# An expert's tokens: rows fetched from DRAM through a slot table and transposed, or columns picked by matrix products

## Chip, cores, metric

One core of a Trainium2 chip. The metric is the device time of one execution in microseconds (us), of three executions; beside it stands one execution taken by the hardware profiler. Engines: TensorE (PE, its weight loads PEld), VectorE (DVE), ScalarE (ACT), GpSimd (POOL), and SyncE (SP), which here only issues transfers. Sixteen DMA engines move the data of all queues.

## The reference, cut to what matters

A decoder of two layers over 256 tokens and 16 meta tokens, D = 1024. The second layer ends in a feed-forward of eight experts, of which each token uses two:

```python
def moe_swiglu(h, router, wg, wu, wd):
    logits = (t @ router).astype(jnp.float32)
    vals, idx = lax.top_k(logits, TOP_K)
    gates = jax.nn.softmax(vals, axis=-1)
    combine = jnp.sum(jax.nn.one_hot(idx, N_EXPERTS) * gates[..., None], 1)
    for e in range(N_EXPERTS):
        out = out + combine[:, e:e + 1] * swiglu(t, wg[e], wu[e], wd[e])
h = layer_norm(ALPHA * h + f, ln2_g[i], ln2_b[i])
```

with `swiglu(t, wg, wu, wd) = (silu(t @ wg) * (t @ wu)) @ wd` and an expert's width of 1408. All is float32; the kernel makes every float32 operand of a product into a high half and a low rest (both float32r) and adds two or three products of halves.

## The kernel before, in words

The first layer, the second layer's mixer and the router fill the time up to about 597 us. From there to about 1064 us the eight experts run one after the other; the change lies there.

**Weights.** An expert has 18 pieces ("units") of up to 1 MB: twelve of the two up products, six of the down product. SP loads them in order (`emit_load`, line 279) into landing buffers called `raw`: four of a ring, and as fifth the tile `yt` once the residual stream in it is done with (line 1562). Four more tiles (`yh`, `yl`, `hid0`, `hid1`, line 1003) serve once, for the first loads of the expert part, before they get their own content. `emit_split` (lines 293 to 327) makes a unit into a high half on ScalarE (line 318) and a low half on VectorE (line 316); after that the landing buffer is free, and the next load can start. Loads wait in SP's queue in the order of issue, so one that waits holds up all behind it.

**Order of the work.** The instructions of PE, DVE, ACT and POOL stand as the program writes them. `product(e, s, ...)` (line 1351) is one of nine phases of an expert: phases 0 to 5 are the up products (`up_proj`), 6 to 8 the down products (`down_proj`). Each takes two units. The lists `todo[e, s]` hold what stands ahead of the product, after a first split, and after a second split. A mask with two bits an expert, read into registers, says how many slots an expert has: at most 64 (one block, high and low half side by side), up to 128, or more, in which case a second block runs under `tc.If` (`second`, line 1165). Experts are sorted by their number of tokens (`order_tables`); with these inputs the third and the sixth have a second block, and the first has one full block. The other five are small.

**Tokens of an expert.** `halve_stream` (line 1246) makes the stream `yt`, 256 rows of 1024, into two tiles `halves_y`. `find` (line 1035) compares the slot numbers with the table `pmk` of each token's slot and gives a matrix of zeros and ones, `hot`. `x_pick` (line 1040) multiplies: for each of eight column blocks and each half, two matrix products of 128x128 by 128x256 give the transposed tokens of all 256 slots in PSUM, exactly, since one factor is one or zero. `x_store` (line 1053) copies them to the tiles `x`. `prepare(e)` (line 1373) spreads these 32 products over phases 4 to 8 of the expert before (`PICKS`). The first expert's tokens are picked in `x_first`, which the change leaves.

**Results.** An expert's rows are written to the DRAM tensor `ys` by POOL (`finish`, line 1500: for a small expert two writes, the second added to the first and waiting for it). At the end `fetch_results` (line 1298) gets each token's rows back by an indirect transfer, and `scale_stream` (line 1318) remakes the stream from the two halves.

```python
    def x_pick(hot, ms, bk):
        for half in range(2):
            for q, m in enumerate(ms):
                for b in range(2):
                    nc.tensor.matmul(ps[:, q, :], halves_y[half][:, b, m * P:(m + 1) * P], hot[:, b, :],
                                     start=(b == 0), stop=(b == 1))
```

Of the kernel before, what the change touches and what calls it, by code (L numbers as in the profile page):

```python
# [11 lines left out]
F32 = mybir.dt.float32  # L12
# [8 lines left out]
P = 128  # L21
# [184 lines left out]
def trunk(ctx, tc, x, meta_tokens, params, consts, selector, rows, weights, out):  # L206
# [156 lines left out]
    ys = dram.tile([2 * (NE - 1) * P, D], F32, name="ys")  # L363

# [47 lines left out]
    def prepare_bias():  # L412
# [559 lines left out]
    def rt(name, dt=F32, w=NE):  # L972
        return wk.tile([P, 2, w], dt, name=name)
# [12 lines left out]
    def y_tile(q):  # L986
        return wk.tile([P, 2, D], F32R, tag=f"y{q}", name=nm("y"), bufs=1)

    def x_tile():
        return wk.tile([P, 2, 2 * P, 2], F32R, tag="x", name=nm("x"), bufs=6)  # L990

    def x_block(xs, s):
        return lambda k: xs[k // 2][:, k % 2, s * P:(s + 1) * P, :]
# [8 lines left out]
    halves_y, hids, got, final = [], [], [], []  # L1002
    spare += [(wk, t, 0) for t in ("yh", "yl", "hid0", "hid1")]
# [6 lines left out]
    def x_first(s, xs):  # L1010
# [9 lines left out]
        for hf in range(2):  # L1020
# [8 lines left out]
            for q in range(2):  # L1029
                halve(raw[:, 2 * q:2 * q + 2, :], xs[2 * hf + q][:, :, s * P:(s + 1) * P, :], P)  # L1030
# [9 lines left out]
    def x_pick(hot, ms, bk):  # L1040

        out = bk.rearrange("p (h m t) -> p h m t", h=2, m=1) if len(ms) == 1 else None
        res = []
        for half in range(2):
            ps = out[:, half] if out is not None else bk[half].rearrange("p (m t) -> p m t", m=2)
            for q, m in enumerate(ms):
                for b in range(2):
                    nc.tensor.matmul(ps[:, q, :], halves_y[half][:, b, m * P:(m + 1) * P], hot[:, b, :],  # L1048
                                     start=(b == 0), stop=(b == 1))
            res.append(ps)  # L1050
        return res

    def x_store(ps, xs, ms):
        dst = xs[ms[0] // 2][:, ms[0] % 2:ms[0] % 2 + len(ms)]
        nc.scalar.activation(dst[:, :, :, 0], ps[0], AF.Copy)
        if len(ms) == 1:
            nc.scalar.activation(dst[:, :, :, 1], ps[1], AF.Copy)
        else:
            vec.tensor_copy(dst[:, :, :, 1], ps[1])


    mask = wk.tile([1, 1], I32, name="mask")
# [590 lines left out]
```

## Time and profile before

| | before |
|---|---|
| median of 3 executions | 1084.95 us (1084.66 to 1088.38) |
| profiled execution | 1084.34 us, span 1082.3 us |
| PE busy | 1024.9 us, 95% of the span |
| DVE busy | 816.9 us, 75% |
| ACT busy | 661.5 us, 61% |
| POOL busy | 29.9 us, 3% |
| moved by DMA | 241.01 MB, mean 223 GB/s |
| SP's weight loads (q1) | 223.72 MB, 56.4% of 16 engines |
| POOL's transfers (q0) | 15.19 MB, 4.2% |

The span runs from the first to the last instruction; the time of an execution has some 2 us more around it. A busy share is an average over stages with different limits, so the expert part is read by stretches. In rows of the trace, "out<-in" names the tiles, "xN" the number of instructions, and an arrow at the end of a row names what ended the idle time before it.

### The profile page before, as it was taken

To read this page: it belongs to the slowest core of one execution; us is meant where nothing else is said; L and a number is where in the kernel's file an instruction comes from. 1 tells how busy PE (TensorE), PEld (TensorE's weight loads), DVE (VectorE), ACT (ScalarE), POOL (GpSimd) and SP (SyncE) were. 2 spreads that over 40 slices of the span, in tenths; PEclk is the share of its full clock that TensorE was granted. 3 is DMA by queue.
4 is the path that set the end of the run, shared out by engine and by line. 5 is a ranking of instruction groups with operands and counts; after the bars stand their busy time and mean duration, and the time that the engine had idled before them with its cause. 6 is when DMAs were issued, how large, how long until landed. Compare 5 with 4: busy or idle time off the path is not lost. (4 is left out here: it accounts for less than half of the span.)

```text
span 1082.3 us, 17618 instructions
## 1 busy us (share of the span) xinstructions
PE 1024.9 (95%) x6619; PEld 926.4 (86%) x6619; DVE 816.9 (75%) x1228; ACT 661.5 (61%) x910; POOL 29.9 (3%) x49
## 2 busy tenths in 40 slices
PE   6999999999999999999999999899998989999895
PEld 3999999899999998989999777789877878978773
DVE  6799977555555545999996998965579995568996
ACT  5348664554544335458566778845569874548983
POOL 0410000000000000000000000000000000000001
PEclk9999999899999999999998999999999999999998
DMA  6962435065455451634346579974679996568994
GB/s 246 320 255 80 155 121 191 1 248 181 157 192 172 153 184 48 226 117 157 117 161 261 203 287 344 390 262 184 231 272 378 396 393 218 190 233 304 383 335 161
DMA packets 37633, 241.01 MB, mean 223 GB/s; under 512 B 4466, under 2 KB 4594, under 8 KB 13952
## 3 DMA queue, kind: packets, MB, share of 16 engines
q1 hardware_dynamic: 33120, 223.72, 56.4%
q0 software_dynamic: 4208, 15.19, 4.2%
q8 instruction: 91, 1.49, 0.5%
q10 hardware_dynamic: 176, 0.29, 0.1%
q14 instruction: 38, 0.31, 0.1%
HBM read 228.41 MB, written 10.77 MB: 221 GB/s over the span
## 5 line engine op out<-in xcount | busy, mean ns | idle before, releaser
L316 DVE TENSOR_TENSOR ws<-raw,ws 128x1024 fp32r<-128x1024 f32 (+3 forms) x307 | 487.5, 1601 | 149.2 <-ACT ws L318 143.7
L318 ACT ACTIVATE ws<-raw 128x1024 fp32r<-128x1024 f32 (+3 forms) x305 | 412.1, 1369 | 109.2 <-PE mm L527 86.1
L527 PE MATMUL mm<-hH,ws 128*128 128x272 f32 (+1 forms) x1568 | 303.2, 290 | 0.0
L527 PEld LDWEIGHTS mm<-hH,ws 128*128 128x128 f32 x1568 | 250.2, 191 | 2.2 <-issue 0.4
L1183 PE MATMUL bank<-ws,x 128*128 128x512 f32 (+1 forms) x1104 | 246.5, 380 | 5.1 <-PEq L1168 4.5
L1183 PEld LDWEIGHTS bank<-ws,x 128*128 128x128 f32 x1104 | 204.0, 192 | 39.7 <-issue 9.3
L527 PE MATMUL mm<-hL,ws 128*128 128x272 f32 (+1 forms) x784 | 226.7, 289 | 0.0
L527 PEld LDWEIGHTS mm<-hL,ws 128*128 128x128 f32 x784 | 149.2, 190 | 0.7
L1183 PE MATMUL bank<-ws,hid 128*128 128x512 f32 x506 | 124.1, 399 | 8.8 <-DVEq L1168 6.8
L1183 PEld LDWEIGHTS bank<-ws,hid 128*128 128x128 f32 x506 | 95.1, 192 | 29.0 <-issue 9.9
L597 DVE SCALAR_TENSOR_TENSOR cbuf<-cbuf,par 128x272 f32<-128x272 f32 (+1 forms) x240 | 106.9, 488 | 0.7
L527 PE MATMUL mm<-fh,ws 128*128 128x272 f32 x352 | 67.1, 289 | 0.0
L527 PEld LDWEIGHTS mm<-fh,ws 128*128 128x128 f32 x352 | 55.3, 188 | 0.1
L1409 ACT ACTIVATE t<-bank 128x512 f32<-128x512 f32 (+1 forms) x48 | 26.6, 554 | 45.1 <-PE bank L1183 43.0
L527 PE MATMUL mm<-fl,ws 128*128 128x272 f32 x176 | 50.6, 287 | 0.0
L527 PE MATMUL mm<-mH,ws 128*128 128x272 f32 (+1 forms) x256 | 49.3, 287 | 0.0
L1048 PE MATMUL bank<-hot,y 128*128 128x256 f32 x224 | 36.0, 292 | 10.7 <-DVE t L1425 6.1
L1048 PEld LDWEIGHTS bank<-hot,y 128*128 128x128 f32 x224 | 30.6, 189 | 16.5 <-DVE t L1425 8.0
L527 PEld LDWEIGHTS mm<-mH,ws 128*128 128x128 f32 x256 | 40.2, 188 | 0.2
L527 PE MATMUL mm<-mL,ws 128*128 128x272 f32 (+1 forms) x128 | 36.3, 285 | 0.0
L527 PEld LDWEIGHTS mm<-fl,ws 128*128 128x128 f32 x176 | 33.1, 188 | 0.0
L1416 PEld LDWEIGHTS bank<-fold,t 128*128 128x128 f32 x220 | 26.9, 191 | 4.0 <-ACTq L1168 2.4
(309 smaller groups left out, 1007.6 us busy)
## 6 DMA issues: line engine op xcount, KB each, us to landing
raw<-in_weights_dram SPq DMA_DIRECT2D x182, 1024.0 KB, 6.0
raw<-in_weights_dram SPq DMA_DIRECT2D x33, 768.0 KB, 6.0
raw<-in_weights_dram SPq DMA_DIRECT2D x8, 512.0 KB, 6.3
ys<-zero POOLq DMA_DIRECT2D x7, 512.0 KB, 12.4
ys<-y POOLq DMA_DIRECT2D x10, 256.0 KB, 6.8
row<-in_rows_dram POOLq DMA_DIRECT2D x2, 1024.0 KB, 7.6
ys<-zero POOLq DMA_DIRECT2D x7, 256.0 KB, 15.5
ys<-y POOLq DMA_DIRECT2D x3, 512.0 KB, 2.9
```

Source lines behind the costliest of these rows:

```text
L316: nc.vector.tensor_sub(lo[:, c0:c1], r[:, c0:c1], h[:, c0:c1].bitcast(F32))
L318: nc.scalar.activation(h[:, c0:c1], r[:, c0:c1], AF.Copy)
L527: nc.tensor.matmul(dst, ww[:, w0:w0 + P], aa[:, ks + i, n0:n1], start=(start and i == 0 and q == 0), stop=(stop and i == len(subs) - 1 and ...
L597: nc.vector.scalar_tensor_tensor(ca[:, c, n0:], src, w, ca[:, c, n0:], op0=ALU.mult, op1=ALU.add)
L1048: nc.tensor.matmul(ps[:, q, :], halves_y[half][:, b, m * P:(m + 1) * P], hot[:, b, :], start=(b == 0), stop=(b == 1))
L1183: nc.tensor.matmul(dst, a, w[:, c0:c1], start=start and q == 0, stop=stop and q == len(terms) - 1)
L1409: nc.scalar.activation(t[q][:, :n], sums[q][:, :n], AF.Copy)
L1416: nc.tensor.matmul(turned[q][:, k * P:k * P + 64], src, fold, start=True, stop=True)
```

## The change

The tokens of the second to the eighth expert are no longer picked by products.

- `keep_stream` writes the stream `yt` to a DRAM tensor `yd` (two writes on POOL, each for 128 tokens).
- `token_table` works out, for each token's two choices, a place in a DRAM table of 8 x 2 x 128 entries, and POOL scatters the tokens' numbers to these places by four indirect transfers; the table was zeroed at the start. It is then read back as `slot_ids`.
- `prepare(e)` has POOL fetch the expert's rows from `yd` by `slot_ids` into the tile `xg`: 64 rows for a small expert, 128 otherwise, and 128 more if there is a second block. TensorE transposes the eight column blocks (`x_turn`, two times four, after phases 6 and 7), and `x_store` halves them on ScalarE and VectorE. For a second block a jump decides on eight more transposes after phase 8 and their halving in the next expert's phase 0.
- `halves_y` and most of the comparisons go. Two tiles `more0`, `more1` are landing buffers that come back after each split. The tiles `x` are now one per block.
- At the end `fetch_stream` reads the stream back from `yd`, and `scale_stream` is one ScalarE instruction per 128 tokens.

```diff
+    yd = dram.tile([SEQ, D], F32, name="yd")
+    table = dram.tile([2 * NE * P, 1], I32, name="table")
...
+        nc.gpsimd.dma_start(table.rearrange("(p c) o -> p (c o)", p=P), zero[:, :2 * NE].bitcast(I32))
...
-    spare += [(wk, t, 0) for t in ("yh", "yl", "hid0", "hid1")]
+    spare += [(wk, t, 0) for t in ("hid0", "hid1")] + [(wk, f"more{i}", 1) for i in range(2)]
...
+    def x_turn(ps, s, hf):
+        for q in range(4):
+            m = 4 * hf + q
+            nc.tensor.transpose(ps[:, q * P:(q + 1) * P], xg[:, s, m * P:(m + 1) * P], ident)
+
+    def x_store(ps, xs, s, hf):
+        halve(ps.rearrange("p (k t) -> p k t", k=4), xs[s][:, 4 * hf:4 * hf + 4], P)
...
+    def token_table():
+        at = rt("at", tag="pos")
+        vec.tensor_scalar(at, pmk, P - BIG, 1.0 - 2 * NE * P, op0=ALU.is_ge, op1=ALU.mult)
+        vec.scalar_tensor_tensor(at, pmk, 2.0 * NE, at, op0=ALU.mult, op1=ALU.add)
+        vec.scalar_tensor_tensor(at, ebase, 2.0 / P, at, op0=ALU.mult, op1=ALU.add)
+        for t in range(2):
+            w, r, ri = rt(f"tw{t}", tag=f"w{t}"), rt(f"tr{t}", w=1, tag=f"gl{t}"), rt(f"ti{t}", dt=I32, w=1)
+            vec.tensor_mul(w, oh[t], at)
+            vec.tensor_reduce(r, w, axis=AX, op=ALU.add)
+            vec.tensor_scalar(r, r, 2.0 * NE * BIG, None, op0=ALU.add)
+            vec.tensor_copy(ri, r)
+            for b in range(2):
+                nc.gpsimd.indirect_dma_start(table, bass.IndirectOffsetOnAxis(ap=ri[:, b, :], axis=0),
+                                             ids[:, b:b + 1], None)
+        nc.gpsimd.dma_start(slot_ids, table.rearrange("(p c) o -> p (c o)", p=P))
...
+    def keep_stream(b):
+        nc.gpsimd.dma_start(yd[b * P:(b + 1) * P, :], yt[:, b, :])
...
+    def fetch_stream():
+        final.append(ring.tile([P, 2, D], F32, tag="yt", name=nm("stream"), bufs=1))
+        nc.gpsimd.dma_start(final[0], yd.rearrange("(b p) d -> p b d", p=P))
...
     def scale_stream(b):
-        high, low = (q[:, b, :].bitcast(F32) for q in halves_y)
-        nc.scalar.activation(stream(b), low, AF.Copy, scale=ALPHA)
-        vec.scalar_tensor_tensor(stream(b), high, ALPHA, stream(b), op0=ALU.mult, op1=ALU.add)
+        nc.scalar.activation(stream(b), stream(b), AF.Copy, scale=ALPHA)
...
+        def gather(s, n):
+            nc.gpsimd.indirect_dma_start(xg[:n, s, :], None, yd, bass.IndirectOffsetOnAxis(
+                ap=slot_ids[:n, 2 * e + s:2 * e + s + 1], axis=0))
...
+        todo[e - 1, 3 if e > 1 else 4][2].append(gathers)
+        for hf in range(2):
+            todo[e - 1, 6 + hf][1].append(lambda hf=hf: turn(hf))
+            todo[e - 1, 7 + hf][0].append(lambda hf=hf: store(hf))
+        todo[e - 1, 8][1].append(turn_second)
+        todo[e, 0][0].append(store_second)
...
+    todo[0, 1][1].append(token_table)
...
-        todo[0, 2 + b][2].append(lambda b=b: halve_stream(b))
+        todo[0, 1 + b][2].append(lambda b=b: keep_stream(b))
...
-        todo[NE - 1, 2 + b][2].append(lambda b=b: scale_stream(b))
+        todo[NE - 1, 4 + b][2].append(lambda b=b: scale_stream(b))
+    todo[NE - 1, 2][2].append(fetch_stream)
```

Where instructions stand, at three places. POOL in the first expert, before: after the loading of two parameter rows there is nothing up to the writing of the first expert's rows, of which the one or the other branch runs.

```order
L1168 UNCONDITIONAL_BRANCH
L1357 UNCONDITIONAL_BRANCH
L1505 REGISTER_ALU
L1505 COMPARE_AND_BRANCH
L1509 DMA ys<-y_7560 64x1024 [waits DMASW0_49,DVE_49,Activation_49]
```

POOL at the same place now; in brackets stand the semaphores that a row waits for (DMASW: POOL's own transfers in turn, DVE, PE, Activation: the engines).

```order
L1166 DMA table<-ids,ti_798_7026 2048x1 [waits DMASW1_49,DVE_49,Pool_49]
L1166 DMA table<-ids,ti_798_7026 2048x1 [waits DMASW2_49,DMASW1_49]
L1166 DMA table<-ids,ti_801_7035 2048x1 [waits DMASW3_49,DMASW2_49,DVE_49]
L1178 UNCONDITIONAL_BRANCH
L1166 DMA table<-ids,ti_801_7035 2048x1 [waits DMASW4_49,DMASW3_49]
L1370 UNCONDITIONAL_BRANCH
L1168 DMA slot_ids<-table 128x16 [waits DMASW5_49,DMASW4_49]
L1257 DMA yd<-yt_last 128x1024 [waits DMASW6_49,DVE_49]
L1257 DMA yd<-yt_last 128x1024 [waits DMASW7_49,DVE_49]
L1392 REGISTER_ALU
L1392 COMPARE_AND_BRANCH
L1387 DMA xg<-yd,slot_ids 64x1024 [waits DMASW6_49,DMASW7_49,DMASW5_49,DMASW0_49]
```

Seven transfers came in ahead of the first gather; each scatter waits for the semaphore of the transfer before it, and the gather for both writes of `yd` and for `slot_ids`.

SP in the first expert, before (raw_7409 goes into `yt`; DMAHW: SP's own transfers in turn):

```order
L279 DMA raw_7273<-in_weights_dram 128x2048 [waits DMAHW7_49,DMAHW3_49,DVE_49]
L1168 UNCONDITIONAL_BRANCH
L1357 UNCONDITIONAL_BRANCH
L279 DMA raw_7409<-in_weights_dram 128x2048 [waits DMAHW4_49,DVE_49,PE_49]
L1357 UNCONDITIONAL_BRANCH
L279 DMA raw_7415<-in_weights_dram 128x2048 [waits DMAHW5_49,DMAHW0_49,DVE_49]
L279 DMA raw_7421<-in_weights_dram 128x1024 [waits DMAHW6_49,DMAHW1_49,DVE_49]
```

SP there now (raw_7180 and raw_7294 go into `more0` and `more1`, raw_7435 into `yt`):

```order
L279 DMA raw_7180<-in_weights_dram 128x2048 [waits DMAHW5_49,DMAHW3_49,DVE_49]
L279 DMA raw_7294<-in_weights_dram 128x2048 [waits DMAHW6_49,DMAHW4_49,DVE_49]
L1392 UNCONDITIONAL_BRANCH
L1178 UNCONDITIONAL_BRANCH
L1370 UNCONDITIONAL_BRANCH
L279 DMA raw_7301<-in_weights_dram 128x2048 [waits DMAHW7_49,DVE_49]
L1370 UNCONDITIONAL_BRANCH
L279 DMA raw_7435<-in_weights_dram 128x1024 [waits DMASW7_49,DMASW6_49,PE_49]
L279 ISA
L279 DMA raw_7441<-in_weights_dram 128x2048 [waits DMAHW0_49,DVE_49]
```

The load into `yt` is now the expert's last unit, two loads later in the order, and waits for POOL's two writes of `yd`.

PE in the third expert, after its seventh product, before (`hot` and `y` are the factors of a pick):

```order
L1169 UNCONDITIONAL_BRANCH
L1168 UNCONDITIONAL_BRANCH
L1048 MATMUL bank_6546<-hot_9486,y_7153 128x256 x4
L1048 MATMUL bank_6543<-hot_9486,y_7154 128x256 x4
L1168 UNCONDITIONAL_BRANCH
L1357 REGISTER_ALU
L1357 COMPARE_AND_BRANCH
```

PE there now (`con` holds the identity matrix, `xg` the fetched rows):

```order
L1179 UNCONDITIONAL_BRANCH
L1178 UNCONDITIONAL_BRANCH
L1044 MATMUL bank_6549<-con,xg 128x128 x4
L1370 REGISTER_ALU
L1370 COMPARE_AND_BRANCH
L1193 MATMUL bank_6545<-ws_9921,hid_9123 128x512
```

Eight products of 256 columns became four transposes of 128; four more stand after the eighth product, and the picks at the other places of the expert are gone.

## Rows read from the trace of the kernel before

**Rows 1.** The cores view of the whole program: span and mean granted TensorE clock.

```profile
core 0: 1082.3 us, clock 0.981
```

**Rows 2.** Table by stretches: length, busy us by engine, granted clock, DMA share, GB/s.

```profile
core 0: us, PE busy (x) PEld busy (x) DVE busy (x) ACT busy (x) POOL busy (x), PEclk, DMA share, GB/s
...
612.00:620.00 8.00, 7.44 (x37) 6.11 (x36) 7.71 (x7) 5.81 (x7) 0.00 (x0) 1.00 0.34 138
620.00:628.00 8.00, 7.28 (x38) 6.41 (x37) 7.97 (x8) 3.49 (x5) 0.00 (x0) 1.00 0.01 2
...
660.00:670.00 10.00, 10.00 (x51) 8.30 (x51) 9.74 (x5) 9.06 (x7) 0.00 (x0) 1.00 0.96 326
...
720.00:797.00 77.00, 76.08 (x394) 65.62 (x393) 44.12 (x53) 40.48 (x46) 1.10 (x2) 1.00 0.58 206
...
860.00:880.00 20.00, 17.49 (x106) 15.47 (x104) 19.14 (x14) 18.35 (x21) 0.00 (x0) 1.00 1.00 394
...
895.00:979.00 84.00, 83.29 (x424) 71.53 (x423) 47.17 (x41) 43.49 (x48) 1.29 (x3) 1.00 0.59 205
...
990.00:1010.00 20.00, 18.04 (x110) 16.26 (x109) 18.68 (x15) 17.30 (x19) 0.00 (x0) 1.00 0.97 389
```

**Rows 3.** The waits of SP's queue, 590 to 1060 us: total, times, longest.

```profile
SPq L279 <- DVE ws L316: 347.2, 118, 18.4
```

**Rows 4.** Line 279's loads, 805 to 895 us: ns, first and last start; landing.

```profile
L279 SPq DMA_DIRECT2D raw<-in_weights_dram x34: 332/333/337, 807.1 to 891.2; - x34
...
DMA to landing us min/median/max: 4.8/7.2/8.8
```

**Rows 5.** The same view, 715 to 795 us.

```profile
DMA to landing us min/median/max: 4.1/4.9/6.2
```

**Rows 6.** Picks of line 1048, third and sixth expert: length, PE, PEld busy.

```profile
705.00:795.00 90.00, 4.60 (x32) 4.45 (x32) 1.00 0.63 227
...
887.00:977.00 90.00, 4.60 (x32) 4.45 (x32) 1.00 0.62 225
```

**Rows 7.** Groups of instructions by form: count, busy us, mean ns, idle before.

```profile
L1048 PE MATMUL bank<-hot,y 128*128 128x256 f32 x224 | 36.0, 292 | 10.7 <-DVE t L1425 6.1 <-issue 3.0 <-PEq L1168 0.9
...
L1059 DVE CAST x<-bank 128x512 fp32r<-128x512 f32 x21 | 14.4, 685 | 0.2 <-PE bank L1183 0.2
...
L1008 DVE TENSOR_TENSOR hid<-t,hid 128x512 fp32r<-128x512 f32 x16 | 11.0, 689 | 0.0
```

**Rows 8.** PE's timeline in the third expert: start, length (us).

```profile
742.57 1.10 PE L1048 MATMUL bank<-hot,y 128*128 128x256 f32 x8
...
747.76 1.04 PE L1418 MATMUL bank<-con,t 128*128 128x128 f32 x8
```

**Rows 9.** VectorE's timeline in the first expert.

```profile
610.80 0.17 DVE L1158 TENSOR_TENSOR chosen<-oh,oh 128x16 f32<-128x16 f32 x1
```

**Rows 10.** The writes of line 1509 (small experts, 0.26 MB), all: landing.

```profile
DMA to landing us min/median/max: 6.3/6.8/7.3
```

**Rows 11.** The writes of line 1511 (0.5 MB), all: landing.

```profile
DMA to landing us min/median/max: 2.9/2.9/7.5
```

**Rows 12.** The indirect fetch of line 1305 (0.5 MB each): landing.

```profile
DMA to landing us min/median/max: 5.2/6.0/6.8
```

**Rows 13.** The row loads of line 1238 (1 MB to all partitions): landing.

```profile
DMA to landing us min/median/max: 6.9/7.6/8.3
```

**Rows 14.** SP's timeline in the first expert.

```profile
627.83 6.28 SPq L279 DMA_DIRECT2D raw<-in_weights_dram  x4
```

**Rows 15.** POOL's timeline at the start of the eighth expert.

```profile
1022.72 0.57 POOL L1509 DMA_DIRECT2D ys<-y  x1 [45.82 <-DVEq L1168]
1029.82 0.86 POOL L1509 DMA_DIRECT2D ys<-y  x1 [6.54 <-DMA ys<-y]
```

**Rows 16.** ScalarE's timeline in the eighth expert.

```profile
1046.60 0.58 ACT L1422 ACTIVATE t<-bank 128x512 f32<-128x512 f32 x1
```

More of the change, by code (lines that the diff above doesn't have):

```diff
@@ L982, in trunk, with x_tiles @@
     ebase = halves(con[:, 3 * P + 16:3 * P + 32])
[L986 to L990, printed above, removed]
+    def x_tiles():
+        return [wk.tile([P, KD, P, 2], F32R, tag=f"x{s}", name=nm("x"), bufs=1) for s in range(2)]
     def x_block(xs, s):
-        return lambda k: xs[k // 2][:, k % 2, s * P:(s + 1) * P, :]
+        return lambda k: xs[s][:, k]
     def hidden_block(hid):
@@ L1038, in find @@
             vec.tensor_scalar(hot[:, b, :], slots0[:, s0:s1], pmk[:, b, e:e + 1], None, op0=ALU.is_equal)
[L1040 to L1059, printed above, removed]
-    mask = wk.tile([1, 1], I32, name="mask")
+    def x_turn(ps, s, hf):
[4 more added lines that the diff above has]
+        halve(ps.rearrange("p (k t) -> p k t", k=4), xs[s][:, 4 * hf:4 * hf + 4], P)
+    mask = wk.tile([1, 1], I32, name="mask")
+    xg = wk.tile([P, 2, D], F32, name="xg")
+    nc.gpsimd.memset(xg, 0.0)
+    ids = wk.tile([P, 2], I32, name="ids")
+    nc.gpsimd.tensor_copy(ids, con[:, POW_AT - 2:POW_AT])
+    slot_ids = wk.tile([P, 2 * NE], I32, name="slot_ids")
     warm = wk.tile([P, 1], F32, name="warm")
@@ L1268, in combine_tables, with look @@
                 vec.tensor_add(glast, glast, gt)
+    def look():
+        hots[NE - 1] = hot_tile()
+        find(hots[NE - 1], NE - 1, 0, 2 * P)
     def double_slots():
@@ L1301, in fetch_results @@
             vec.tensor_copy(rowi[t], rowf[t])
-            got.append([wk.tile([P, D], F32, tag="x", name=nm("got"), bufs=6) for _ in range(2)])
+            g = wk.tile([P, 2, D], F32, tag=f"x{t}", name=nm("got"), bufs=1)
+            got.append([g[:, b] for b in range(2)])
         for b in range(2):
@@ L1339, in trunk @@
     todo = {(e, s): ([], [], []) for e in range(NE + 1) for s in range(9)}
-    xts = {0: [x_tile() for _ in range(4)]}
+    xts = {0: x_tiles()}
     hots = {}
-    xps = {}
     ys_t = {}
@@ L1367, in product, with gathers, turn, store @@
                 f()
[L1370 to L1371 removed]
     def prepare(e):
[L1375 to L1392 removed]
+        bits = 2 * e
+        def gather(s, n):
+            nc.gpsimd.indirect_dma_start(xg[:n, s, :], None, yd, bass.IndirectOffsetOnAxis(
+                ap=slot_ids[:n, 2 * e + s:2 * e + s + 1], axis=0))
+        def gathers():
+            v = sizes[(E.Pool,)]
+            with tc.If((v & (3 << bits)) == 0) as few:
+                gather(0, 64)
+            with few.Else():
+                gather(0, P)
+                with tc.If((v & (2 << bits)) != 0):
+                    gather(1, P)
+        def turn(hf):
+            if hf == 0:
+                xts[e] = x_tiles()
+            x_turn(bank(e - 1, 6), 0, hf)
+        def store(hf):
+            x_store(bank(e - 1, 6), xts[e], 0, hf)
+        def turn_second():
+            with tc.If((sizes[(E.PE,)] & (2 << bits)) != 0):
+                for hf in range(2):
+                    x_turn(bank(e - 1, 2 * hf), 1, hf)
+        def store_second():
+            with tc.If((sizes[(E.Activation, E.DVE)] & (2 << bits)) != 0):
+                for hf in range(2):
+                    x_store(bank(e - 1, 2 * hf), xts[e], 1, hf)
+        todo[e - 1, 3 if e > 1 else 4][2].append(gathers)
+        for hf in range(2):
+            todo[e - 1, 6 + hf][1].append(lambda hf=hf: turn(hf))
+            todo[e - 1, 7 + hf][0].append(lambda hf=hf: store(hf))
+        todo[e - 1, 8][1].append(turn_second)
+        todo[e, 0][0].append(store_second)
     def expert(e):
@@ L1552, in trunk @@
     todo[2, 2][2].append(combine_tables)
+    todo[NE - 1, 0][1].append(look)
     todo[NE - 1, 0][1].append(double_slots)
```

31 lines of the change are left out of this document (4 added, 27 removed).

## The prediction

> **What bounds the kernel now.** I read the cores view first: one core, 1082.3 us at a granted clock of 0.981 [rows 1]. So the clock is near the upper of its two levels, and no term below comes from it. Next comes the table by stretches of the expert part, which runs from 597 us on [rows 2]. The reader is to see two kinds of stretch. In the third and the sixth expert (720 to 797, 895 to 979 us) TensorE is busy for 76.08 of 77 and 83.29 of 84 us while the DMA share is 0.58 and 0.59: there TensorE sets the pace. In the short experts between and after them (660 to 670, 860 to 880, 990 to 1010 us) the DMA share is 0.96 to 1.00, and TensorE is busy for 17.49 of 20 us in the second of these: there the weight transfers set the pace. I call these DMA-bound stretches A (632 to 710), B (805 to 895) and C (985 to 1050). In the first expert, 612 to 628 us, the transfers almost stop (0.34, then 0.01).
>
> Why they stop is in the waits of SP's queue: the weight loads of line 279 waited 347.2 us, in 118 waits, for VectorE's split of line 316, which gives a landing buffer back [rows 3]. So a load starts when a buffer is free, five can be under way or waiting (four of the ring and the tile `yt`), and every long expert ends with five loaded. In B, 34 loads begin between 807.1 and 891.2 us, 2.55 us apart, and land after 7.2 us [rows 4]; in the third expert, with the engines half idle, after 4.9 us [rows 5].
>
> **The change, part by part.** The picks: 224 matmuls, 36.0 us busy [rows 7], 32 for each of the seven prepared experts. What that is worth depends on the stretch. In the third and the sixth expert the 32 picks take 4.60 us each [rows 6], and TensorE has nothing else to wait for. In their place stand eight transposes of 128x128; eight such take 1.04 us [rows 8], and the second block's eight are jumped over in these two, since the experts prepared there are small. That is 2 x (4.60 - 1.04) = 7.1 us gained. The new jumps on TensorE I put at 0.2 us in all; the bounds are 0 (most jumps of before leave no gap in the rows) and 2. In the other five preparations the saving is TensorE time in a DMA-bound stretch: I cost it at nothing, the cover being the weight transfers. Without that cover it would be the second rival.
>
> ScalarE and VectorE: the casts of line 1059 (21 of 685 ns) [rows 7], their ScalarE halves, the comparisons of `look` and the halving of the stream go; two halvings per block, of 689 ns on VectorE [rows 7], and eleven short instructions for the table come. All this lies beside TensorE in the long experts and beside the transfers in the short ones: nothing, and at most about 1 us an expert if both covers went.
>
> Two buffers more: `more0` and `more1` come back for use after every split, where `yh` and `yl` served once, so seven loads instead of five. A DMA-bound stretch then begins with two loads more done in the idle time before it: 2 x 2.55 = 5.1 us in each of A, B, C.
>
> New transfers in the same stretches. 64 rows of 4 KB are 0.26 MB, 256 rows 1.05 MB; at 394 GB/s [rows 2] 0.7 and 2.7 us. B: gathers for the fifth and sixth experts, 3.4 us. C: for the eighth, 0.7, and the stream read back, 2.7: 3.4 us. A: for the second and third, 3.4 us. So B and C each give 5.1 - 3.4 = 1.7 us. The remaining gathers fall in long experts, where the engines have room.
>
> Stretch A has one more step, on POOL. The table's four scatters write the same DRAM tensor, so each waits on POOL until the one before it has landed; behind them on POOL stand the read of the slot numbers, the two writes of the stream, and the first gather. Behind the stream's writes stands SP: the load into `yt`, the eighteenth of the expert part, waits for them, and every later load is behind it in SP's queue. The time: VectorE ends the reordered tables at 610.97 us [rows 9]; seven short instructions of about 0.2 us give the first indices at 612.4. A link of the chain lies between 2.9 us (the quickest write of before, in a long expert [rows 11]) and 7.3 us (the slowest small one, in the short experts [rows 10]). The nearest row is the indirect fetch at the end: 5.2 to 6.8 us for 0.5 MB of rows behind others [rows 12]; with almost no bytes I take 4.0, plus 0.3 to go on. Four links end at 629.6; two issues of about 0.6 bring the stream's writes to 630.8, and at 6.9 us, the quicker of the two row loads of the same 1 MB [rows 13], they land at about 638. Before, four loads went out from 627.83 us on within 6.28 us [rows 14]. Now two go out earlier, one there, and then the queue stands. The engines run dry at about 634 and carry weights again 4.9 - 2.55 = 2.3 us after 638 [rows 4, 5]: 6 us lost against 5.1 gained. With the gathers, A costs 0.9 + 3.4 = 4.3 us. Bounds: links of 2.9 and a landing of 2.9 us end at 629.2, nothing stands, A gives 1.7; links of 7.3 are the first rival. The first gather itself comes some 6 us after 638, and TensorE may stand for it; in A that delays nothing the transfers have not delayed.
>
> Last, the share: A runs at 0.96, C at 0.97 [rows 2]. With seven loads it should go to 1.00: 3% of some 65 us, 2 us; bounds 0 and 3.
>
> **Sum**: 7.1 - 0.2 - 4.3 + 1.7 + 1.7 + 2 = 8.0 us. The profiled execution took 1084.34 us, 0.6 under the median of 1084.95, so the forecast is 1076.3, say 1076.
>
> **The rivals.** *The chain on POOL is slow, and the kernel gets slower.* Each scatter takes what a small write takes in the short experts, 7.3 us [rows 10], and the stream's writes 7.5: 612.4 + 4 x 7.6 + 1.2 + 7.5 = 651.5 us. SP's queue stands from 634 to 653.8, some 20 us; A then costs 20 - 5.1 + 3.4 = 18 us and the sum turns to 6 us slower, 1090. It decides from a landing at about 646 us on, links of 6.2 us. For it: POOL's writes of 6.8 us fall where VectorE is nearly always busy, and from 612 to 628 it is (7.71 of 8 and 7.97 of 8 us [rows 2]). Against it: the transfers are idle then, and idle transfers go with 2.9 us. The trace does not separate the two.
> [...]
>
> *TensorE is the bound everywhere.* Then all picks count: 36.0 - 9 x 1.04 = 26.6 us, 1058. For it: TensorE is busy nearly 90% of the time even in the short experts. Against it: the DMA share of 1.00 there, which a faster TensorE doesn't change.
>
> *The stream comes back late.* On POOL its fetch stands behind the two writes of the seventh expert's rows, issued at 1022.72 and, after 6.54 us of waiting for the first, at 1029.82 us [rows 15]; with as long for the second it goes out at about 1037 and lands by about 1045. ScalarE reaches the scaling behind the copies of 1046.60 us [rows 16], just later. If two more loads under way make each of the three transfers 5.1 us longer, it lands at 1060; the last splits wait behind the scaling on ScalarE, and the end moves by about 8 us: 1084.
> [...]
>
> **How the numbers follow.** Forecast 0.55, slow chain 0.17, TensorE everywhere 0.12, late stream 0.12, anything else 0.04. About 0.5%, 5.4 us, is what a measurement of this kernel tells from no change: faster is below 1079.5, slower above 1090.4. The forecast's own ends are 1070 (quick chain) and 1082 (links of 5.5 us, no gain in share); most of it and all of the second rival are faster: 0.60. Slower are half of the first rival and the rest: 0.12. The same: 0.28. The range, 1064 to 1090, leaves out the second rival's end and the first one's upper half.
>
> **What would show it.** Right: weight loads under way between 612 and 628 us, where the share was 0.01; in the third and sixth expert no line 1048 and about 3.5 us less each; the gap of SP's queue before the eighteenth load ending with the stream's writes, at about 638 us; the DMA share at 1.00 in all of A, B, C. Wrong: links under 3 or over 6 us; a ScalarE wait for the fetched stream near 1040 us; a DMA share below 0.95 in a short expert, which would say that the transfers were not the bound; or transposes that wait for a gather in a long expert.

## The result, and the profile after

The changed kernel took 1094.2 us, median of six executions (1092.14 to 1098.06); the kernel before, in six beside it, 1087.54 (1084.66 to 1088.47). The ratio is 1.0070, with a 95% interval of 1.0047 to 1.0093: slower by 0.7%, above the range's end of 1090. The cores view of the changed kernel (span, mean granted TensorE clock), where [rows 1] had 1082.3 and 0.981:

```profile
core 0: 1093.8 us, clock 0.968
```

Where the time went is read from tables whose borders are the first up product of each expert, so a row is an expert from start to start. First the kernel before (the third and the sixth row are the long experts; the last is the end):

```profile
core 0: us, PE busy (x) PEld busy (x) DVE busy (x) ACT busy (x) POOL busy (x), PEclk, DMA share, GB/s
597.28:657.47 60.19, 55.40 (x265) 45.88 (x265) 54.87 (x55) 43.07 (x44) 0.54 (x1) 1.00 0.68 256
657.47:702.61 45.14, 40.34 (x219) 34.60 (x217) 42.16 (x31) 40.22 (x39) 0.53 (x1) 1.00 0.98 369
702.61:793.53 90.92, 90.00 (x452) 77.20 (x452) 52.86 (x57) 45.07 (x50) 1.97 (x3) 1.00 0.64 231
793.53:838.28 44.75, 40.72 (x218) 34.72 (x217) 41.65 (x30) 39.67 (x39) 0.53 (x1) 1.00 0.92 337
838.28:884.26 45.98, 40.82 (x216) 34.57 (x216) 43.46 (x31) 40.81 (x41) 1.43 (x2) 1.00 1.01 393
884.26:975.04 90.78, 90.07 (x452) 77.26 (x452) 50.92 (x42) 44.71 (x50) 1.98 (x3) 1.00 0.64 230
975.04:1019.80 44.76, 40.73 (x217) 34.67 (x217) 41.62 (x30) 39.72 (x39) 0.53 (x1) 1.00 0.91 344
1019.80:1065.57 45.77, 41.07 (x196) 34.30 (x196) 42.28 (x42) 36.45 (x41) 6.30 (x7) 0.93 0.85 307
1065.57:1082.30 16.73, 5.79 (x16) 2.86 (x16) 10.31 (x20) 3.77 (x7) 0.00 (x0) 0.81 0.39 150
```

The same table of the changed kernel:

```profile
596.06:664.99 68.93, 54.39 (x241) 44.62 (x241) 52.58 (x61) 40.09 (x38) 12.26 (x9) 0.93 0.72 265
664.99:712.30 47.31, 40.08 (x200) 33.42 (x200) 44.30 (x30) 39.46 (x36) 4.93 (x3) 0.96 0.99 390
712.30:801.08 88.78, 87.19 (x429) 74.06 (x429) 50.60 (x54) 43.51 (x45) 3.04 (x4) 1.00 0.62 223
801.08:848.05 46.97, 39.99 (x194) 32.99 (x193) 43.07 (x28) 38.05 (x34) 2.50 (x3) 0.93 0.99 375
848.05:895.36 47.31, 41.17 (x200) 33.97 (x201) 42.69 (x28) 39.04 (x37) 6.88 (x5) 0.93 1.00 390
895.36:984.18 88.82, 87.23 (x429) 74.06 (x429) 48.58 (x39) 44.05 (x46) 2.72 (x4) 1.00 0.62 221
984.18:1031.04 46.86, 39.80 (x194) 33.24 (x193) 43.08 (x28) 38.00 (x34) 2.29 (x2) 0.93 0.99 377
1031.04:1072.80 41.76, 37.89 (x196) 31.78 (x196) 37.35 (x39) 35.27 (x41) 7.13 (x8) 1.00 0.74 276
1072.80:1093.80 21.00, 8.31 (x16) 3.96 (x16) 11.10 (x21) 3.90 (x8) 0.00 (x0) 0.71 0.38 147
```

The reader is to see four things. The first expert is 8.74 us longer. The four short ones between (second, fourth, fifth, seventh) are 2.17, 2.22, 1.33 and 2.10 us longer, although TensorE has no more work in them than before; their granted clock is 0.93 to 0.96 where it was 1.00. The two long ones are 2.14 and 1.96 us shorter. The eighth with the end is 0.26 longer (4.01 shorter itself, the end 4.27 longer; why they shift so was not followed), and the start is 1.22 earlier. The sum is 11.5 us, the difference of the two spans. These are single executions; the interval of the ratio allows 5 to 10 us.

What happened in the first expert stands in POOL's timeline (start, length, instruction, and in brackets the idle time before it and what ended that) of the changed kernel:

```profile
611.96 3.02 POOL L1166 DMA_INDIRECT table<-ids,ti  x1 [10.37 <-issue]
616.67 1.00 POOL L1166 DMA_INDIRECT table<-ids,ti  x1 [1.69 <-DMA table<-ids,ti]
619.60 1.91 POOL L1166 DMA_INDIRECT table<-ids,ti  x1 [1.93 <-DVE ws L316]
626.17 1.67 POOL L1166 DMA_INDIRECT table<-ids,ti  x1 [4.66 <-DMA table<-ids,ti]
633.23 0.59 POOL L1168 DMA_DIRECT2D slot_ids<-table  x1 [5.40 <-DMA table<-ids,ti]
633.81 1.10 POOL L1257 DMA_DIRECT2D yd<-yt_last  x2
639.44 2.45 POOL L1387 DMA_INDIRECT xg<-yd,slot_ids  x1 [4.53 <-DMA yd<-yt_last]
```

The chain of four scatters, the read of the slot numbers and the stream's writes ends with the first gather at 639.44. Two others wait for this chain. SP's queue, in its waits (total, times, longest):

```profile
SPq L279 <- DMA yd<-yt_last: 11.3, 1, 11.3
```

And TensorE, in its timeline: the first transposes come 9.09 us after TensorE had nothing else to do.

```profile
649.64 1.09 PE L1044 MATMUL bank<-con,xg 128*128 128x128 f32 x4 [9.09 <-DMA xg<-yd,slot_ids]
```

The gathers' landings (line 1387). The trace has three of the nine, of which the first, 0.26 MB, is the longest with 10.06 us:

```profile
DMA to landing us min/median/max: 7.1/9.5/10.1
```

The weight loads from 812 to 895 us landed after 4.4, 8.7 and 11.4 us (shortest, median, longest), where [rows 4] had 4.8, 7.2 and 8.8.

In the long experts the eight transposes that took the place of the 4.60 us of picks [rows 6] (length, PE, PEld busy of line 1044):

```profile
712.00:800.00 88.00, 1.20 (x8) 0.99 (x8) 1.00 0.62 224
```

The end of a short expert, here the fifth, in TensorE's timeline: the last down product behind its wait.

```profile
885.23 0.66 PE L1044 MATMUL bank<-con,xg 128*128 128x128 f32 x4 [1.54 <-DVE ws L316]
888.35 5.46 PE L1193 MATMUL bank<-ws,hid 128*128 128x512 f32 x12 [2.46 <-DVE hid L1008]
```

The same in slices of 2 us, with the granted clock ahead of the last two numbers. In slices of half a us it is 1.00 or 0.50 throughout the spans of both kernels, but for the slices in which it changes; here it falls from 1.00 to 0.50:

```profile
884.00:886.00 2.00, 0.66 (x4) 0.42 (x4) 2.00 (x3) 0.69 (x2) 0.00 (x0) 1.00 0.99 414
886.00:888.00 2.00, 0.00 (x0) 0.00 (x0) 2.00 (x2) 1.88 (x3) 0.00 (x0) 0.77 1.00 418
888.00:890.00 2.00, 1.65 (x4) 1.39 (x5) 1.77 (x3) 2.00 (x2) 0.00 (x0) 0.50 1.01 410
```

In the kernel before (its timeline, then a slice), picks stood in this gap, and the same twelve products ran at a granted clock of 1.00:

```profile
877.79 1.10 PE L1048 MATMUL bank<-hot,y 128*128 128x256 f32 x8
880.67 3.03 PE L1183 MATMUL bank<-ws,hid 128*128 128x512 f32 x12 [1.77 <-DVEq L1168]
```

```profile
880.00:882.00 2.00, 1.33 (x6) 1.14 (x7) 1.74 (x3) 2.00 (x3) 0.00 (x0) 1.00 1.04 418
```

TensorE waited before them in both kernels; with the picks the clock stayed at 1.00, without them the products took 5.46 us instead of 3.03, and the copy of the expert's rows waits for them. ScalarE's wait ahead of that copy (total, times, longest), in the fifth expert before and now:

```profile
ACT y L1225 <- PE bank L1183: 0.4, 1, 0.4
```

```profile
ACT y L1235 <- PE bank L1193: 2.5, 1, 2.5
```

It was 0.4 us in each of the four short experts and is 1.5, 2.4, 2.5 and 2.5: 7.3 us more, where the four are 7.8 us longer.

### The profile page after: what moved, and what is told of

The parts are those of the page before. It is cut to its first block, busy times and chain, and to the rows that moved or that the text cites. A ratio compares the mean times of both kernels' runs of the same rounds, so it can differ in the third digit from the quotient of the medians.

```text
span 1093.8 us, 17400 instructions
## 1 busy us (share of the span) xinstructions
PE 1014.2 (93%) x6467; PEld 910.7 (83%) x6467; DVE 810.1 (74%) x1220; ACT 648.7 (59%) x877; POOL 61.1 (6%) x69
## 5 line engine op out<-in xcount | busy, mean ns | idle before, releaser
L318 ACT ACTIVATE ws<-raw 128x1024 fp32r<-128x1024 f32 (+3 forms) x305 | 407.3, 1367 | 98.7 <-PE mm L530 86.3
L1193 PE MATMUL bank<-ws,x 128*128 128x512 f32 (+1 forms) x1104 | 243.5, 378 | 13.3 <-PEq L1178 5.1
L1193 PE MATMUL bank<-ws,hid 128*128 128x512 f32 x506 | 135.6, 423 | 15.3 <-DVE hid L1008 10.5
L1193 PEld LDWEIGHTS bank<-ws,hid 128*128 128x128 f32 x506 | 101.8, 206 | 39.9 <-issue 16.5
L1007 ACT ACTIVATE hid<-t 128x512 fp32r<-128x512 f32 (+3 forms) x30 | 17.9, 597 | 32.5 <-DVE t L1455 28.9
L1007 ACT ACTIVATE x<-bank 128x512 fp32r<-128x512 f32 x18 | 11.0, 625 | 38.8 <-PE bank L1044 38.7
L1008 DVE TENSOR_TENSOR x<-bank,x 128x512 fp32r<-128x512 f32 x18 | 12.2, 688 | 27.0 <-ACT x L1007 24.5
```

The costliest lines, as they stand in the source:

```text
L318: nc.scalar.activation(h[:, c0:c1], r[:, c0:c1], AF.Copy)
L1007: nc.scalar.activation(dst[:, :, :n, 0], src, AF.Copy)
L1008: vec.tensor_sub(dst[:, :, :n, 1], src, dst[:, :, :n, 0].bitcast(F32))
L1193: nc.tensor.matmul(dst, a, w[:, c0:c1], start=start and q == 0, stop=stop and q == len(terms) - 1)
```

## The experiments

Theory: the first expert waits twice, SP's queue for the stream's writes and TensorE for the first gather; and in the short experts the pace has passed from the transfers to VectorE and TensorE, whose clock falls where the picks stood. Its rival is the prediction's view: the weight transfers set the pace there, and what TensorE waits for only shows it. A ratio is taken against runs of the kernel before on the same chip, and runs are compared with each other by their ratios (the changed kernel's is 1.0070); edits are to the changed kernel unless said otherwise.

### The first expert: late transposes, early writes, both

`late_turn` moves the first preparation's transposes behind the first expert's last product:

```diff
+        if e == 1:
+            todo[0, 8][1].append(turn_late)
+            todo[1, 0][0].extend((store_late, turn_second, store_second))
+            return
         for hf in range(2):
             todo[e - 1, 6 + hf][1].append(lambda hf=hf: turn(hf))
```

> The first preparation's eight transposes move behind the first expert's last product, onto two free banks; all else is the changed kernel. Theory 1 (stall): in the changed kernel TensorE stood 9.09 us for the first gather, its clock then fell to 0.50, and the first expert took 68.93 us instead of 60.18. If that wait on TensorE is the whole loss there, the first expert goes back to 60 to 62 us and the time falls by 7 to 9 us, to about 1086. Theory 2 (transfers): the first expert is long because SP's queue and the row transfers stand; the wait on TensorE only shows it. Then the wait moves behind the last product, the first two experts together gain at most 2 us, and the time stays at 1092 or more.

1091.62 us, ratio 1.0055 (1.0036 to 1.0075), which noise doesn't tell from the changed kernel's: what theory 2 expected. The wait for the gather is gone from TensorE, but the first expert is at 66.00, not at 60 to 62, and the second at 49.20 where it was 47.31, so the two gain 1.0 us together. ScalarE's timeline shows what is late next, the weights themselves, since the load was held back until 641.44; of its four waits for a load, 8.6 us, the longest is:

```profile
645.18 1.06 ACT L318 ACTIVATE ws<-raw 128x1024 fp32r<-128x1024 f32 x1 [3.53 <-DMA raw<-in_weights_dram]
```

`early` puts the stream's writes between the scatters on POOL, when their halves are ready:

```diff
+        scatter_ids(0, 0)
+        scatter_ids(0, 1)
...
+    def read_ids():
+        scatter_ids(1, 1)
         nc.gpsimd.dma_start(slot_ids, table.rearrange("(p c) o -> p (c o)", p=P))
...
         todo[0, 1 + b][2].append(lambda b=b: keep_stream(b))
+        todo[0, 1 + b][2].append(read_ids if b else lambda: scatter_ids(1, 0))
```

> The changed kernel with another order on POOL: the stream's two writes go out between the scatters, as soon as VectorE has the halves ready (about 617 and 624 us, instead of 633.81 and 634.37 behind all four scatters and the read of the slot numbers). The 18th weight load, which waited for them until 638.70, can go at about 629, and so can all behind it; the first gather then waits only for the slot numbers, and goes out at about 636.5 instead of 639.44. Theory 1 (two waits, the queue of SP and TensorE's wait for the gather, each of which costs by itself): the loads are on time again, but the gather has to land among them, after 8 to 10 us, and TensorE still stands for 5 to 7 us; the first expert takes 65 to 67 us and the time is 1088 to 1092. Theory 2 (all of the first expert's loss is SP's queue): the first expert goes back to 60 to 61 us, and the time to about 1086.

1094.01 us, ratio 1.0076 (1.0048 to 1.0103): no gain, short of theory 1's 1088 to 1092 and far from theory 2's 1086. SP's queue now waits for the writes no more than 1.1 us (SP's waits), and the eighteenth load landed at 636.27:

```profile
SPq L279 <- DMA yd<-yt_last: 1.1, 1, 1.1
```

TensorE's waits, and the first expert's row of the table by experts: the gather is waited for as long as before, and the expert takes as long as ever.

```profile
PE bank L1044 <- DMA xg<-yd,slot_ids: 10.0, 1, 10.0
```

```profile
596.24:665.70 69.46, 54.12 (x240) 44.40 (x241) 52.54 (x61) 40.03 (x38) 11.72 (x9) 0.93 0.71 263
```

`early_late` has both edits.

> Both at once: the stream's writes early on POOL, and the first preparation's transposes behind the first expert's last product. Theory 1 (two waits, either of which is enough to hold the first expert up): neither is left, the first expert takes 60 to 62 us, the second no more than 47, and the time is 1084 to 1087. Theory 2 (the table's transfers and the gathers cost because of their bytes in the queues, wherever they stand): the first two experts together gain less than 4 us against the changed kernel, and the time stays above 1089.

1085.62 us, ratio 1.0006 (0.9992 to 1.0021), level with the kernel before. Its first two experts:

```profile
596.18:655.32 59.14, 52.22 (x240) 42.74 (x241) 53.79 (x62) 40.67 (x38) 10.91 (x10) 1.00 0.81 299
655.32:704.20 48.88, 42.78 (x200) 35.36 (x200) 43.15 (x29) 38.34 (x35) 4.18 (x4) 0.90 1.01 410
```

So either wait alone holds the first expert up. The first two experts took 116.2 us in the changed kernel, 115.2 and 116.6 with one of the waits removed and 108.0 with both; by the ratios both together are worth about 7 us. The second expert did not keep under 47.

### The clock: unread products, and half of the picks

`warm` puts work into the gap:

```diff
             def down(blocks, st, d=d):
+                for i in range(14 if st and d == 2 and not last else 0):
+                    nc.tensor.matmul(bank(e, 0)[:, :256], hid[0][:, 0, :, 0],
+                                     hid[0][:, 0].rearrange("p t h -> p (t h)"), start=True, stop=True)
```

> The changed kernel with 14 products of 256 columns, whose result nobody reads, ahead of the last down product of every small expert, where TensorE waited 2.46 us for the last hidden half and its clock went from 1.00 to 0.50. Theory 1 (clock): the 12 hidden products behind it took 5.46 us there against 3.03 us before, and all that follows at the expert's end waits for them. With the clock kept up they take about 3.0 again, each of the four short experts (46.9 to 47.3 us) loses 1.5 to 2.4 us, and the time falls by 6 to 9 us, to 1085 to 1088. Theory 2 (transfers or VectorE set the pace of a short expert): the products then only wait elsewhere, the short experts stay at 47 us, and the time is 1094 within 1 us.

1091.16 us, ratio 1.0048 (1.0031 to 1.0066): 2.4 us less by the ratios, a third of what was expected, and not clear of noise, since the intervals overlap. The mean granted clock did rise: 0.974 to 0.979 in the ten executions, where the six of the changed kernel had 0.968 or 0.969. In the trace the last down product is back at 3.0 us in all four short experts. The second expert came back to 45.37 at a clock of 1.00 and the seventh to 44.40; in the fourth, fifth and seventh the clock now fell to 0.50 around the first down product instead, which took 5.50, 5.51 and 5.51 us, and the fifth, at 48.53, is longer than without the added products.

`half_picks` is the kernel before, with a loop `for b in range(1)` in `x_pick` in place of `range(2)`.

> The kernel before with half of its picks (those of the second 128 tokens) left out, so the prepared experts' tokens are incomplete. It takes 16 products away from each preparation and nothing else. Theory 1 (clock): the third and sixth expert gain 2 x 2.3 us, but with TensorE less busy its clock falls at the end of the short experts as in the changed kernel, which costs up to 2 us in each of four: 1083 to 1090, with granted clocks below 1.00 in the short experts. Theory 2 (the clock is no matter of the picks): 4.6 us faster, 1080 to 1083, and the granted clock stays at 1.00.

1086.55 us, ratio 1.0009 (0.9998 to 1.0020). The 4.6 us that TensorE saves in the long experts are there (about 1.8 of 2.3 in each), and are lost in the short ones: the second goes from 45.14 to 49.62, the fourth from 44.75 to 46.35, while the fifth and seventh move by half a us down and up. The second, its row and then slices at its end:

```profile
657.81:707.43 49.62, 42.51 (x202) 35.02 (x200) 44.90 (x33) 40.76 (x40) 0.53 (x1) 0.93 0.96 359
```

```profile
700.00:702.00 2.00, 0.01 (x1) 0.00 (x0) 2.00 (x2) 1.83 (x2) 0.00 (x0) 0.97 1.02 414
702.00:704.00 2.00, 1.73 (x4) 1.47 (x5) 1.74 (x2) 2.00 (x3) 0.00 (x0) 0.50 0.94 360
```

Nothing but picks was taken from the kernel before, and in the second and the fourth expert its clock falls at the place where the changed kernel's does, to 0.50 and 0.55 in slices of 2 us; in the seventh it fell at the first down product, to 0.50, and in the fifth not at all. Over the whole program the mean granted clock was 0.973 to 0.977 in its ten executions, against 0.978 to 0.984 in the 21 of the kernel before beside them. So the picks kept the clock up, though half of them were still enough in one of the four.

### What sets the pace of a short expert: buffers, splits, bytes

`five`: the two added buffers serve once.

```diff
-    ... + [(wk, f"more{i}", 1) for i in range(2)]
+    ... + [(wk, f"more{i}", 0) for i in range(2)]
```

> The changed kernel with the two added landing buffers used once, as the two of the kernel before were, so five loads can be under way instead of seven. Theory 1 (the transfers did not bind in the changed kernel, whose loads landed 2 to 9 us ahead of their split): the same time within 2 us, 1092 to 1096. Theory 2, the prediction's (every short stretch starts with two loads more done): 3 x 5.1 us slower, about 1109; a part of it, 4 us or more, if they bind in some stretches.

1104.13 us, ratio 1.0174 (1.0152 to 1.0197): 10 to 11 us slower than the changed kernel, so theory 1 was wrong here. With five loads under way the transfers do bind, and most where the large gathers stand, in the second expert (49.52 us where it was 47.31) and the fifth, where ScalarE waits four times for a load, 5.9 us (the fifth's row, then ScalarE's waits there). The fourth and the seventh, with one small gather each, are only 0.15 and 0.21 us longer.

```profile
850.91:902.50 51.59, 42.64 (x201) 35.30 (x201) 42.78 (x28) 39.20 (x37) 5.78 (x5) 0.90 0.98 374
```

```profile
ACT ws L318 <- DMA raw<-in_weights_dram: 5.9, 4, 2.9
```

This run also shows what made POOL's chain slow. With fewer buffers, SP's queue stood for the stream's writes from an earlier load on, 25.7 us, so the last two scatters went out beside almost no loads:

```profile
623.03 2.47 POOL L1166 DMA_INDIRECT table<-ids,ti  x1 [1.59 <-DMA table<-ids,ti]
626.96 0.59 POOL L1168 DMA_DIRECT2D slot_ids<-table  x1 [1.45 <-DMA table<-ids,ti]
```

The third and the fourth link, from start to start, are 3.72 and 3.93 us here and 6.57 and 7.06 in the changed kernel. From 620 to 628 us VectorE was busy for 7.50 of 8 us here and 7.58 there, but the DMA share was 0.02 here and 0.58 there.

`half_low` and `half_load` ask of the kernel with seven loads what sets the pace.

```diff
+                skip = u % 2 and (u - moe_units) // expert_units in (1, 3, 4, 6) and u >= moe_units
...
-            subs += [(h, lo, (k - k0) * n) for k in range(k0, k1)]
+            subs += [(h, h if skip else lo, (k - k0) * n) for k in range(k0, k1)]
```

> The changed kernel with VectorE's split left out for every second unit of the four short experts (the high half is taken again in its place, so these experts' results are wrong in their low parts). It takes some 9 instructions of 1.2 to 2.3 us, 19 us, from VectorE in each short expert; transfers, TensorE and ScalarE keep their work. Theory 1 (VectorE, with TensorE waiting for what it makes, sets the pace of a short expert, and no longer the transfers): the short experts go from 47 to 43 or 44 us, where the transfers bind at 17.3 MB and about 400 GB/s; time 1080 to 1084. Theory 2 (the transfers set the pace, as the prediction had it): the short experts stay at 46 to 47 us, time 1091 to 1094.

```diff
+        if (first_units - len(units) - 1) // expert_units in (1, 3, 4, 6):
+            nc.sync.dma_start(raw[:, :K * n // 2], source(off, K, n)[:, :K * n // 2])
```

> The changed kernel with half of the weight bytes left out in the four short experts (each unit's first half is loaded and used twice, so their results are wrong). The engines keep all of their work. Theory 1 (the transfers are no longer what a short expert waits for): the short experts stay within 1 us of 47, the whole time within 3 us of 1094, the first expert's wait apart. Theory 2 (the transfers set the pace): the short experts fall by several us each, to 43 us or less, and the time to 1080 or less.

Half the splits: 1078.72 us, ratio 0.9937 (0.9913 to 0.9961), under theory 1's range. Half the bytes: 1096.65 us, ratio 1.0109 (1.0082 to 1.0137), no faster than the changed kernel. The fourth expert of the one and of the other, where the changed kernel had 46.97 us at a clock of 0.93 and a DMA share of 0.99:

```profile
792.74:835.97 43.23, 39.62 (x193) 33.12 (x193) 25.39 (x19) 38.54 (x34) 1.48 (x2) 0.92 1.00 391
```

```profile
801.13:848.22 47.09, 40.12 (x194) 32.97 (x193) 43.07 (x28) 38.03 (x34) 2.44 (x3) 0.93 0.65 204
```

With less for VectorE it falls by 3.7 us, though its clock falls just as far (its last down product took 5.46 us); the second expert, whose clock stayed at 1.00, falls by 5.6. With half the weights to bring, 204 GB/s and a share of 0.65, the expert stays where it was. In the changed kernel the transfers do not set the pace of a short expert: VectorE's work does, and TensorE's clock behind the last hidden half adds to it.

### The versions that beat both

`best` and `best_b` are `early_late` with unread products ahead of the first and the last down product of small experts, 14 and 14 or 6 and 18 (the loop of `warm`, with `range((6, 0, 18)[d] ...)`). `nojump` is `early_late` with the second block's transposes and halvings fixed to the third and sixth expert; `all_three` is `best_b` with that. In these two the other experts also keep one tile for the second block, so the edit is not the jumps alone.

```diff
-            with tc.If((sizes[(E.PE,)] & (2 << bits)) != 0):
-                for hf in range(2):
-                    x_turn(bank(e - 1, 2 * hf), 1, hf)
+            for hf in range(2 if e in (2, 5) else 0):
+                x_turn(bank(e - 1, 2 * hf), 1, hf)
```

> The stream's writes early and the first transposes late, as in the run before this one with both (1085.62 us), and on top of it products that nobody reads, 14 of 256 columns ahead of the first and 14 ahead of the last down product of each small expert. Theory 1 (clock): in that run the granted clock fell to 0.50 around the last down product of all four short experts, whose 12 products took 5.46, 5.46, 4.32 and 4.56 us instead of 3.03; with TensorE kept at work through the waits of 1.2 and 2.7 us ahead of them, the short experts lose 1.3 to 2.4 us each, 5 to 7.6 us in all, and the time is 1078 to 1081, faster than both kernels. Theory 2 (VectorE alone sets the pace of a short expert, at 42 to 43 us of work in 46 to 47): the products come back but VectorE's line does not get shorter, at most 1 us an expert is won, and the time is 1082 to 1085.

> The same with 6 such products ahead of the first and 18 ahead of the last down product, since the deepest fall was ahead of the last one. Theory 1: like the kernel with 14 and 14 or up to 2 us better, 1077 to 1081; if the clock falls ahead of the first down product instead, as it did with 14 ahead of the last alone, up to 3 us worse. Theory 2: 1082 to 1085.

> The kernel with the stream's writes early and the first transposes late (1085.62 us) without the added jumps for a second block: its transposes and halvings stand in the program for the third and the sixth expert alone, where these inputs need them. It measures the jumps, which the prediction put at 0.2 us in all, with 0 and 2 as bounds. Theory 1 (jumps cost next to nothing): 1084 to 1086. Theory 2 (each added jump, on ScalarE and VectorE too, holds up the expert's start, where TensorE waited 0.56 to 1.49 us behind one): 0.5 to 1 us for each of seven experts, 1079 to 1082.

> All three at once: the stream's writes early with the first transposes late, 6 and 18 unread products ahead of the first and the last down product of the small experts, and no added jumps (the second block's transposes stand for the third and the sixth expert alone, so this version holds for inputs with these two large experts). Theory 1 (three losses of their own: the wait for the first gather, the clock, the jumps): the gains add, 1085.6 - 6.4 (unread products) - 3.8 (no jumps), about 1075 to 1077. Theory 2 (jumps and clock hold up the same moments at an expert's end): the smaller gain is already in the larger one, 1078 to 1080.

Measured: `best` 1083.88 us, 0.9981 (0.9968 to 0.9995); `best_b` 1079.26, 0.9947 (0.9928 to 0.9965); `nojump` 1081.8, 0.9963 (0.9949 to 0.9977); `all_three` 1080.59, 0.9951 (0.9932 to 0.9970). So `best_b`, which still decides at run time on the second blocks, is faster than both kernels by 0.5% and 1.2%. `best_b` and `nojump` came where their clock and jump theories had them; `best` came in theory 2's range. Where the products stand matters: with 14 and 14 the clock still fell to 0.50 in the middle of the fourth and the seventh expert, and the fifth, at a clock of 1.00, took 46.30 us where `early_late` had 46.43. The fourth and the fifth expert of `best_b`, where the changed kernel had 46.97 and 47.31 at 0.93:

```profile
792.55:836.91 44.36, 40.12 (x217) 34.44 (x217) 41.27 (x27) 37.53 (x34) 2.29 (x2) 1.00 0.99 376
836.91:882.80 45.89, 41.27 (x224) 35.14 (x225) 42.72 (x28) 39.52 (x37) 4.34 (x4) 1.00 1.00 396
```

Against the kernel before, the short experts of `best_b` are between 0.4 us shorter and 1.2 longer; its gain stands in the two long ones, 2 us each, and in the first and the eighth, 1.2 and 3.2 us, while the start and the end are 1.2 us longer each.

Taking out the jumps is worth 4 to 5 us by itself (1.0006 to 0.9963) and nothing on top of `best_b`. That fits theory 2 of the last expectation, jumps and clock holding up the same moments, but no row shows it: the profiled execution of `nojump` (1085.49 us) was one of its slowest. How the two divide the gain is open.

## Why the prediction was wrong

**The chain on POOL.** Forecast: links of 4.3 us, the writes landed at 638, SP's queue standing for 6 us. Measured: links of 4.71, 2.93, 6.57 and 7.06 us, an end 3.6 us later, and writes that landed at 638.63 all the same, since they took 4.3 us and not 6.9. Two errors cancelled, which was luck. The queue stood for 11.3 us, from an earlier start, because the two loads more had gone ahead as forecast.

**The step that failed first** is "The first gather itself comes some 6 us after 638, and TensorE may stand for it; in A that delays nothing the transfers have not delayed", at a cost of nothing. All of A was put at 4.3 us; the first expert alone lost 8.74. The gather took 10.06 us and landed at 649.50; TensorE stood for 9.09 us and its clock fell to 0.50. `early` had the weights there and lost as much; only `early_late` won the time back. Two waits at one place were taken for one because they overlap: the later one counts in full as soon as the earlier one is gone.

**The step that failed second** is "In the other five preparations the saving is TensorE time in a DMA-bound stretch: I cost it at nothing". It was a loss of 7.8 us: without the picks TensorE stood in the fifth expert for 1.54 and 2.46 us ahead of the last down product, with 0.66 us of transposes between, where it had stood once for 1.77; the clock falls to 0.50 at the end of each short expert, and four experts are 1.3 to 2.2 us longer. `half_picks` and `best_b` show it, and so does ScalarE's wait for the slow product. The prediction had set the clock aside for one mean of 0.981 ("no term below comes from it").
The cover was misread too. Already in the kernel before, VectorE was busier in the short experts than TensorE (19.14 and 18.68 of 20 us [rows 2]; 43.46 of 45.98 in the fifth), and ScalarE waited little for weights. In its waits in the fifth expert before (total, times, longest):

```profile
ACT ws L318 <- DMA raw<-in_weights_dram: 1.5, 2, 0.9
```

In the second it waited 0.8 us for a load, in the fourth and the seventh not at all. No run brings fewer bytes in the kernel before.

**Two buffers more, 5.1 us in each of A, B and C.** Without them the kernel loses 10 to 11 us (`five`) where the three terms make 15: by the rows 2.8 us in the first two experts, 4.4 in the fourth and fifth, and under 1 in the seventh, eighth and the end. But no gain is left against the kernel before. By the places of the loss they pay for the large gathers; beyond that VectorE sets the pace, which the prediction did not price: it is busy for 42.7 to 44.3 us of 47 in these experts.

**The DMA share** went to 0.99 to 1.00 in the four short experts, as forecast, and the 2 us did not come: `half_load` brings half the weights and is no faster. A share near 1 said that loads were under way, not that somebody waited for them.

**The long experts**: 2.14 and 1.96 us won instead of 3.56 each. The picks' 4.60 us became 1.20, 3.4 less; the rest was given back within the expert, in TensorE's idle time, 1.6 us against 0.9, and in its busy time, which fell by 2.8 us and not 3.4 (the rows by expert).

**The jumps on TensorE**, 0.2 us with bounds of 0 and 2, an estimate that no row gave: taken out by themselves, on three engines, they give 4 to 5 us, so the price of an added jump was too low; what TensorE's own jumps cost no run shows.

**The rivals.** The slow chain did not come by its own condition, a landing from 646 us on (it was 638.63), though the time is near its 1090: right time, another wait. Its links did come, 6.57 and 7.06 us in the chain's second half.
A busy VectorE, which spoke for this rival in the prediction, is not what made the links slow: from 620 to 628 us it was busy for 7.50 us in `five` and 7.58 in the changed kernel, and the links took 3.72 and 3.93 us at a DMA share of 0.02 in the one and 6.57 and 7.06 at 0.58 in the other. Nor did the gathers on POOL slow VectorE: the split of line 316 took 2289 ns in the second expert before and 2288 now.
TensorE as the bound everywhere is refuted: it is busy for 436.06 us in this part instead of 444.94, and the part is longer. The late stream was not waited for: it landed at 1049.70, and ScalarE came to the scaling at 1054.13.

**The forecast's upper end**, 1082, does not follow from its terms: links of 5.5 us instead of 4.0 or 4.3 add 5 to 6 us and the missing gain in share 2, which makes 1083 to 1084.

## What to carry to other kernels

Price a new wait as if it were the only one: two that overlap hide each other, in the forecast and in an experiment that removes one. Before leaving out work on TensorE that seems free, look at the granted clock and at the waits beside it, since that work may be what keeps the clock up: with half of the picks gone it fell to 0.50 in the second expert. Whether a stretch is bound by transfers is told by what the splits wait for and by halving the bytes, not by the busy share: this was 0.99 in the fourth expert, which took 46.97 us, and 47.09 with half the bytes.

## What was not expected of the hardware

Products that nobody reads made the kernel faster: with 96 of them more, `best_b` is at 0.9947 where `early_late` is at 1.0006. A gather of 64 rows of 4 KB took 10.06 us to land beside seven weight loads, longer than a write of 0.26 MB in the short experts before, beside five at most (6.3 to 7.3 us [rows 10]). A scatter of 128 numbers took 3.72 and 3.93 us a link with the transfers nearly idle (a DMA share of 0.02), and 6.57 and 7.06 beside weight loads (0.58). And a scatter or a gather held POOL for 1.0 to 3.1 us at its issue, a plain transfer for 0.5 to 1.0.
